# A buffer of their own for layer 0's modulation rows, and four temporaries in place of six

## The chip, the cores and the metric

The kernel runs on one core of a Trainium2 chip. The metric is the device time of one execution, in microseconds (us), as the median of several executions. The engines are named as in the profile: PE (TensorE's matmuls), PEld (its weight loads), DVE (VectorE), ACT (ScalarE), POOL (GpSimd) and SP (SyncE, which issues all the loads and stores here). L129 means line 129 of the kernel.

## What is computed

A bidirectional encoder of two layers over 1024 tokens of width 1024, in float32. Layer 0 mixes tokens by differential attention with 8 heads, layer 1 by grouped-query attention; each has a SwiGLU block behind it. Every norm is modulated by a condition vector: six rows of 1024 numbers per layer come from a product with a large matrix. Cut to layer 0's first half:

```python
cond = silu(c)
mod = (cond @ ada_w[i] + ada_b[i])          # 6 x 1024 per layer
shift1, scale1, gate1, shift2, scale2, gate2 = split(mod, 6)
h = rmsnorm(x, norm1_g[i]) * (1 + scale1) + shift1
q, k, v = split(h @ w_qkv, 3)               # 8 heads; q and k have two halves of 64
q, k = rope(q), rope(k)                     # the first quarter of each half is rotated
w = softmax(q1 k1) - lam * softmax(q2 k2)
y = rmsnorm(w @ v, subln_g) * (1 - lam_init) @ w_o
x = x + gate1 * y
```

## The kernel before

Activations lie as 8 blocks of 128 features by 1024 tokens, worked on in chunks of 512 tokens. A float32 product is made of three matmuls: each operand is split into a rounded high part and the low rest (`split`, L94: a cast on ACT, a subtraction on the engine named, POOL in layer 0 for weights). `weights` (L82) loads a raw tile of 128x1024 (tag `wraw`), then splits it into `whi` and `wlo`; the pool `wp0` has two buffers for each of the three tags.

`start` (L334) loads x and the first two modulation rows' matrices (`aq`, reduced on DVE at L377), normalises x, and projects q, k and v of head 0. `layer0_attn` (L439) then runs 8 heads of 8 query blocks (a head's 64 units are walked by `attention`, L272). While head h is in its scores, softmax and values, the projections of head h+1 are mixed in as fills: six groups of 24 matmuls (`qkv_steps`, L474: q, k and v, two chunks each), each in the one PSUM bank M, which ACT empties at L470 (`evac`) into a temporary `tmp`. For q and k, `rope_fin` (L457) takes a second temporary, shuffles the first into it on DVE (L221), multiplies by the tables and adds (L223 to L225, on POOL for heads above 0), and `pack` splits the result into two tiles of the pool `h`. That pool has 50 tiles of 128x512: 32 hold the layer's input throughout the projections, 8 each the rotated q and k of a head. `subln` (L568) takes two more temporaries for the norm of the output of each half head; the second is stored to memory by SP (L1050).

The other four modulation rows of layer 0 (gate1, scale2, shift2, gate2) are made during the heads by `ada_steps` (L121): 32 steps, four or five to a head, in the fills of heads 0 to 6. A step loads 128x1024 of the matrix, multiplies it by the condition on POOL (L129) and sums it on ACT (L130). Its tile is also a `wraw` of `wp0`, so weights and steps share two buffers. Layer 1 calls the same function.

No order is written out by hand: a planner in the framework goes through the program with its own model of time and writes the list of each engine, taking the instruction of highest priority that is ready; priorities follow the program, lifted for some (`high_priority`). Buffers of a tag are given out in program order, an engine works through its list in order, and SP's list is the order of all the loads and stores.

Of the kernel before, what the change touches and what calls it, by code (L numbers as in the profile page):

```python
# [9 lines left out]
F32 = mybir.dt.float32  # L10
# [44 lines left out]
SH_A = [i ^ 8 if i < 16 else i for i in range(32)]  # L55
# [3 lines left out]
class Trunk:  # L59
# [58 lines left out]
        self.nc.scalar.activation(out=t, in_=t, func=AF.Silu)  # L118
        return t

    def ada_steps(self, layer, j, dst, cond):  # L121

        nc = self.nc

        def step(d):
            w = self.t(self.wp, "wraw")
            nc.sync.dma_start(out=w, in_=self.a["ada_t"][layer, j - 2, d])
            with self.tc.high_priority(offset=DAHEAD):
                nc.gpsimd.tensor_tensor(out=w, in0=w, in1=cond, op=ALU.mult)  # L129
                nc.scalar.activation(out=w, in_=w, func=AF.Copy, accum_out=dst[:, d:d + 1])  # L130
            if d == KT - 1:
                b = C_ADAB + layer * 48 + j * 8
                nc.gpsimd.tensor_tensor(out=dst, in0=dst, in1=self.sm[:, b:b + 8], op=ALU.add)

        return [lambda d=d: step(d) for d in range(KT)]
# [303 lines left out]
    def layer0_attn(self, hs, tiles, od):  # L439
        nc, tc, a = self.nc, self.tc, self.a  # L440
        m = self.mods[0]
        self.wlo = nc.gpsimd
        with tc.tile_pool(name="a_tab", bufs=1, reuse_waits="tile") as tab, \
                tc.tile_pool(name="a_v", bufs=2, reuse_waits="tile") as vp, \
                tc.tile_pool(name="a_tmp", bufs=6, reuse_waits="tile") as tp, \
                tc.tile_pool(name="a_e", bufs=5, reuse_waits="tile") as ep, \
                tc.tile_pool(name="a_p", bufs=6, reuse_waits="tile") as pp:
            cos, sin = self.t(tab, "cos"), self.t(tab, "sin")
# [6 lines left out]
            half = lambda: self.t(tp, "tmp", [P, CH])  # L455

            def rope_fin(h, i, c, z):  # L457
                cs = slice(c * CH, c * CH + CH)
                self.rope(half(), z, cos[:, cs], sin[:, cs], SH_A, z, nc.gpsimd if h else None)
                ready.setdefault((h, i), []).append(self.pack(z))  # L460

            def evac(h, i, c, ps):
                if i == 2:
                    if c == 0:
                        vt[h] = self.t(tab, "vz")
                    z = vt[h][:, c * CH:(c + 1) * CH]
                else:
                    z = half()
                with self.tc.high_priority(offset=MAHEAD):
                    nc.scalar.activation(out=z, in_=ps, func=AF.Copy, scale=0.125 if i == 0 else 1.0)  # L470
                if i < 2:
                    rope_fin(h, i, c, z)
# [19 lines left out]
            ada = []  # L492
            cond = self.condr
            for j in (2, 4, 3, 5):
                ada += self.ada_steps(0, j, m[j], cond)
            fills = []
            wo = self.wo = OutProj(self, a["woA"], od, a["xT"], m[2])
            for h in range(8):
# [704 lines left out]
```

## Time and profile before

| | us |
|---|---|
| median of 3 runs | 2755.31 (2752.56 to 2761.1) |
| profiled execution | 2753.28 |
| its span, first to last instruction | 2751.2 |
| mean granted TensorE clock | 0.97 of full speed |

| engine | busy, share of the span |
|---|---|
| PE | 95% |
| PEld | 78% |
| DVE | 70% |
| ACT | 43% |
| POOL | 36% |

The start lasts until about 72 us, layer 0's heads until about 735 us; then follow layer 0's SwiGLU block, layer 1's heads from about 1480 us and its SwiGLU block. A busy share is a mean over these stages. For a change in one stage, the idle time of PE in that stage is what counts: the stretches of the span give it, and the single instructions show what ended each wait.

### The profile page before, as it was taken

To read this page: it belongs to the slowest core of one execution; us is meant where nothing else is said; L and a number is where in the kernel's file an instruction comes from. 1 tells how busy PE (TensorE), PEld (TensorE's weight loads), DVE (VectorE), ACT (ScalarE), POOL (GpSimd) and SP (SyncE) were. 2 spreads that over 40 slices of the span, in tenths; PEclk is the share of its full clock that TensorE was granted. 3 is DMA by queue.
4 is the path that set the end of the run, shared out by engine and by line. 5 is a ranking of instruction groups with operands and counts; after the bars stand their busy time and mean duration, and the time that the engine had idled before them with its cause. 6 is when DMAs were issued, how large, how long until landed. Compare 5 with 4: busy or idle time off the path is not lost.

```text
span 2751.2 us, 34376 instructions
## 1 busy us (share of the span) xinstructions
PE 2600.1 (95%) x12888; PEld 2138.1 (78%) x12888; DVE 1913.9 (70%) x2921; ACT 1193.2 (43%) x2049; POOL 988.7 (36%) x664
## 2 busy tenths in 40 slices
PE   6799999999998999999999899999998999999997
PEld 5577777777776888888887788888877888888886
DVE  6777777777667667676666777577567666666666
ACT  5455555555443333333334565555443333332323
POOL 7634444531154223232223456433153222222222
PEclk9899999999998999999999999999999999999998
DMA  6211211112211222221214222213211111111112
GB/s 255 74 44 49 70 50 59 63 42 96 78 49 58 66 65 74 65 69 62 71 64 146 96 73 89 85 59 110 70 35 50 54 50 58 54 50 54 50 58 85
DMA packets 86582, 195.89 MB, mean 71 GB/s; under 512 B 9488, under 2 KB 11792, under 8 KB 86416
## 3 DMA queue, kind: packets, MB, share of 16 engines
q1 hardware_dynamic: 86416, 193.71, 20.7%
q8 instruction: 101, 1.65, 0.3%
q14 instruction: 65, 0.53, 0.1%
HBM read 177.94 MB, written 15.73 MB: 70 GB/s over the span
## 4 chain that ended last, share of the span: by engine, by line
PE 76%; DVE 12%; ACT 3%; POOL 3%; DMA 2%; issue 2%; SPq 0%; DVEq 0%; ACTq 0%; POOLq 0%
PE T L105 7%; PE T L106 7%; PE T L107 7%; PE S L106 6%; PE S L105 6%; PE S L107 6%; PE M L105 6%; PE M L106 5%; PE M L107 5%; PE S L548 3%; PE T L256 3%; PE A L270 2%; PE A L268 2%; PE A L269 2%; DVE mx L556 2%
## 5 line engine op out<-in xcount | busy, mean ns | idle before, releaser
L833 POOL TENSOR_TENSOR raw<-raw,raw 128x512 f32<-128x512 f32 x214 | 299.2, 1399 | 877.5 <-DMA raw<-in_w_in 552.1
L95 ACT CAST whi<-raw 128x512 fp32r<-128x512 f32 x402 | 249.0, 621 | 672.1 <-PE T L106 215.7
L96 DVE TENSOR_TENSOR wlo<-raw,whi 128x512 fp32r<-128x512 f32 x402 | 330.3, 826 | 124.8 <-ACT whi L95 124.4
L105 PE MATMUL M<-h,whi 128*128 128x512 f32 x616 | 252.6, 410 | 8.6 <-ACT tmp L470 4.2
L1036 DVE SCALAR_TENSOR_TENSOR h<-T,mod,h 128x512 f32<-128x512 f32 (+1 forms) x270 | 197.7, 733 | 70.8 <-PE T L107 69.6
L107 PE MATMUL M<-h,wlo 128*128 128x512 f32 x616 | 244.6, 397 | 1.0 <-POOL wlo L96 1.0
L105 PE MATMUL S<-h,whi 128*128 128x512 f32 x572 | 226.7, 397 | 19.5 <-DVE ft L918 19.3
L106 PE MATMUL M<-h,whi 128*128 128x512 f32 x616 | 244.9, 398 | 0.0
L95 ACT CAST pt<-T 128x512 fp32r<-128x512 f32 x256 | 145.3, 588 | 211.5 <-PE T L256 211.0
L106 PE MATMUL S<-h,whi 128*128 128x512 f32 x572 | 227.5, 398 | 5.0 <-DVE h L214 3.1
L96 DVE TENSOR_TENSOR pt<-T,pt 128x512 fp32r<-128x512 f32 x256 | 171.6, 682 | 80.7 <-ACT pt L95 80.4
L107 PE MATMUL S<-h,wlo 128*128 128x512 f32 x572 | 226.2, 396 | 0.0
L105 PE MATMUL T<-g,whi 128*128 128x512 f32 (+1 forms) x540 | 210.7, 390 | 10.2 <-DVE h L1036 8.8
L106 PE MATMUL T<-g,whi 128*128 128x512 f32 (+1 forms) x540 | 208.3, 386 | 1.4 <-DVE g L96 1.4
L107 PE MATMUL T<-g,wlo 128*128 128x512 f32 (+1 forms) x540 | 207.9, 385 | 0.0
L129 POOL TENSOR_TENSOR wraw<-wraw,cond 128x1024 f32<-128x1024 f32 x64 | 155.9, 2437 | 126.9 <-DMA wraw<-in_ada_t 119.6
L556 DVE TENSOR_REDUCE mx<-S 128x1 f32<-128x1024 f32 x128 | 150.2, 1215 | 44.3 <-PE S L548 44.2
L270 PE MATMUL A<-pt,v 128*128 128x256 f32 x512 | 155.6, 304 | 23.2 <-DVE pt L96 23.2
L559 ACT ACTIVATE e<-S,mx 128x1024 f32<-128x1024 f32 x128 | 141.4, 1111 | 71.7 <-DVE mx L558 71.7
L256 PE MATMUL T<-ident,e 128*128 128x128 f32 x1024 | 149.1, 280 | 13.3 <-DVE pt L96 10.1
L268 PE MATMUL A<-pt,v 128*128 128x256 f32 x512 | 156.3, 305 | 4.3 <-ACT pt L95 4.2
L269 PE MATMUL A<-pt,v 128*128 128x256 f32 x512 | 151.4, 296 | 0.0
(290 smaller groups left out, 6445.7 us busy)
## 6 DMA issues: line engine op xcount, KB each, us to landing
raw<-in_w_in SPq DMA_DIRECT2D x200, 256.0 KB, 2.8
wraw<-in_ada_t SPq DMA_DIRECT2D x64, 512.0 KB, 3.2
raw<-in_w_out SPq DMA_DIRECT2D x88, 256.0 KB, 2.6
wraw<-in_wqkvA SPq DMA_DIRECT2D x23, 512.0 KB, 3.2
aq<-in_ada_s SPq DMA_DIRECT2D x16, 512.0 KB, 4.9
raw<-in_ada_w SPq DMA_DIRECT2D x32, 256.0 KB, 2.6
wraw<-in_wqkvB SPq DMA_DIRECT2D x15, 512.0 KB, 3.3
o<-tmp SPq DMA_DIRECT2D x28, 256.0 KB, 2.0
```

The costliest lines, as they stand in the source:

```text
L95: self.nc.scalar.copy(out=hi, in_=src)
L96: (eng or self.nc.vector).tensor_tensor(out=lo, in0=src, in1=hi.bitcast(F32), op=ALU.subtract)
L105: mm(ps, lhsT=whi[:, ws], rhs=xh, start=first and k == 0, stop=False)
L106: mm(ps, lhsT=whi[:, ws], rhs=xl, start=False, stop=False)
L107: mm(ps, lhsT=wlo[:, ws], rhs=xh, start=False, stop=last and k == n - 1)
L256: nc.tensor.transpose(ps[:, i * P:(i + 1) * P], w[:, k * P:(k + 1) * P], self.ident)
L268: mm(ps, lhsT=vh[:, ks], rhs=hi, start=(k == 0), stop=False)
L269: mm(ps, lhsT=vl[:, ks], rhs=hi, start=False, stop=False)
L270: mm(ps, lhsT=vh[:, ks], rhs=lo, start=False, stop=(k == KT - 1))
L556: nc.vector.tensor_reduce(out=mx, in_=ps, op=ALU.max, axis=AX.X, negate=True)
L833: self.nc.gpsimd.tensor_tensor(out=t, in0=x, in1=y, op=op)
L1036: self.nc.vector.scalar_tensor_tensor(out=x, in0=ps, scalar=gate2[:, d:d + 1], in1=x, op0=ALU.mult, op1=ALU.add)
```

## The change

The 32 steps of layer 0 take their tiles from the pool `cr`, which held only the condition's row, under a tag of its own with one buffer (4 KB per partition). The weights and the loads of stored outputs keep the two `wraw` buffers. The pool of temporaries of layer 0's attention has four buffers instead of six (4 KB per partition less). The second tile of a rotation comes from the pool `h` instead. Layer 1 is as before.

```diff
-    def ada_steps(self, layer, j, dst, cond):
+    def ada_steps(self, layer, j, dst, cond, pool=None):
 ...
-            w = self.t(self.wp, "wraw")
+            w = self.t(pool, "adaw") if pool else self.t(self.wp, "wraw")
             nc.sync.dma_start(out=w, in_=self.a["ada_t"][layer, j - 2, d])
 ...
-                tc.tile_pool(name="a_tmp", bufs=6, reuse_waits="tile") as tp, \
+                tc.tile_pool(name="a_tmp", bufs=4, reuse_waits="tile") as tp, \
 ...
-                self.rope(half(), z, cos[:, cs], sin[:, cs], SH_A, z, nc.gpsimd if h else None)
+                self.rope(self.hslot(F32), z, cos[:, cs], sin[:, cs], SH_A, z, nc.gpsimd if h else None)
 ...
-                ada += self.ada_steps(0, j, m[j], cond)
+                ada += self.ada_steps(0, j, m[j], cond, self.cpool)
```

## Rows read from the trace of the kernel before

**Rows 1.** The page, part 1: busy us, share of the span, instructions.

```profile
PE 2600.1 (95%) x12888; PEld 2138.1 (78%) x12888; DVE 1913.9 (70%) x2921; ACT 1193.2 (43%) x2049; POOL 988.7 (36%) x664
```

**Rows 2.** Stretches: bounds, length, busy PE, PEld, DVE, ACT, POOL; clock, DMA share, GB/s.

```profile
35.00:72.00 37.00, 35.20 (x139) 26.86 (x140) 28.55 (x63) 14.56 (x21) 28.91 (x16) 0.95 0.49 172
72.00:135.00 63.00, 46.23 (x205) 33.56 (x205) 49.14 (x63) 31.84 (x54) 45.24 (x23) 0.86 0.22 76
135.00:293.00 158.00, 152.42 (x887) 122.81 (x887) 117.13 (x201) 85.22 (x150) 64.06 (x41) 0.96 0.14 51
```

**Rows 3.** The same stretches, L129 alone: bounds, length, POOL busy; clock, DMA.

```profile
35.00:72.00 37.00, 2.40 (x1) 0.95 0.49 172
72.00:135.00 63.00, 14.68 (x6) 0.86 0.22 76
```

**Rows 4.** Instructions on tile wraw, both layers: ns min/median/max, first and last start.

```profile
L129 POOL TENSOR_TENSOR wraw<-wraw,cond x64: 2348/2392/3347, 43.3 to 1862.5; 128x1024 f32<-128x1024 f32 x64
L130 ACT ACTIVATE wraw<-wraw x64: 1043/1060/1086, 48.3 to 1865.0; 128x1024 f32<-128x1024 f32 x64
L130 ACT ACTIVATION_READ_ACCUMULATOR wraw<-wraw x64: 182/186/217, 49.2 to 1866.0; 128x1 f32 x64
...
DMA to landing us min/median/max: 2.6/3.2/10.2
```

**Rows 5.** Timeline of the start: start, us, instruction, [idle before <- what ended it].

```profile
34.99 4.61 POOL L388 TENSOR_SCALAR nh<-h,a,mod 128x512 f32<-128x512 f32 x2 [1.80 <-DVE mod L379]
...
42.06 0.68 DVE L389 TENSOR_TENSOR h<-nh,h 128x512 fp32r<-128x512 f32 x1
...
43.33 2.88 DVE L389 TENSOR_TENSOR h<-nh,h 128x512 fp32r<-128x512 f32 x1 [0.53 <-POOL nh L388]
...
43.27 2.40 POOL L129 TENSOR_TENSOR wraw<-wraw,cond 128x1024 f32<-128x1024 f32 x1
...
51.33 0.50 PE L106 MATMUL S<-h,w0h 128*128 128x512 f32 x1 [0.69 <-DVE h L389]
...
72.55 1.77 POOL L223 TENSOR_TENSOR tmp<-tmp,cos 128x512 f32<-128x512 f32 x1 [4.27 <-DVE tmp L221]
```

**Rows 6.** Timeline of SP's queue in the start.

```profile
34.73 0.38 SPq L127 DMA_DIRECT2D wraw<-in_ada_t  x1
...
49.42 0.38 SPq L86 DMA_DIRECT2D wraw<-in_wqkvA  x1
```

**Rows 7.** Timeline of SP's queue and of ACT, head 1: a weight.

```profile
181.65 0.33 SPq L86 DMA_DIRECT2D wraw<-in_wqkvA  x1
...
193.45 1.05 ACT L95 CAST whi<-wraw 128x1024 fp32r<-128x1024 f32 x1 [0.16 <-PE M L106]
```

**Rows 8.** Timeline of DVE, ACT and PE in the run-in.

```profile
80.05 1.63 DVE L96 TENSOR_TENSOR h<-tmp,h 128x512 fp32r<-128x512 f32 x1
...
86.24 0.62 ACT L95 CAST h<-tmp 128x512 fp32r<-128x512 f32 x1 [7.42 <-DVE tmp L225]
86.77 0.59 ACT L470 ACTIVATE tmp<-M 128x512 f32<-128x512 f32 x1
...
87.41 0.51 PE L105 MATMUL M<-h,whi 128*128 128x512 f32 x1 [2.60 <-ACT tmp L470]
```

**Rows 9.** Two half heads: all engines as in rows 2, then L129 alone.

```profile
336.50:376.80 40.30, 38.65 (x224) 31.51 (x224) 30.34 (x55) 22.99 (x40) 21.64 (x14) 0.96 0.14 46
...
455.60:495.50 39.90, 37.97 (x217) 30.16 (x216) 32.36 (x47) 20.86 (x37) 16.39 (x10) 0.96 0.22 73
...
336.50:376.80 40.30, 3.92 (x2) 0.96 0.14 46
...
455.60:495.50 39.90, 7.90 (x4) 0.96 0.22 73
```

**Rows 10.** Waits of ACT from 135 to 608: us in total, times, longest.

```profile
ACT h L95 <- POOL tmp L225: 8.3, 4, 5.0
```

**Rows 11.** Waits of DVE from 0 to 72: us in total, times, longest.

```profile
DVE aq L377 <- DMA aq<-in_ada_s: 1.2, 1, 1.2
```

## The prediction

> **What bounds the kernel now.** I read the page's busy shares first, then stretches of the span, then the single instructions at the places that the change touches. TensorE is busy for 95% of the span [rows 1], so an edit that touches no matmul can only move TensorE's idle time. Layer 0's attention phase ends near 735 us; everything the change touches lies before that. By stretch [rows 2], TensorE idles 37.00 - 35.20 = 1.8 us in the second half of the start (35 to 72), 63.00 - 46.23 = 16.8 us in the run-in (72 to 135, head 0's rotation and first scores), and 5.6 us in the 158 us behind that. Only the run-in is a place with something to win; the start is a place with almost no cover: whatever becomes late there is late on TensorE.
>
> The modulation rows are 32 loads of 512 KB, each followed by one POOL multiply (L129) and one ACT sum (L130). Of the 32, one is multiplied before 72, six in the run-in [rows 3], and the other 25 behind that. Now they take turns with the q, k, v weights in two buffers, in the order of the program, so a row can't run ahead of the weights.
>
> **Part 1: what the weights gain from their two buffers: nothing.** A weight load issued at 181.65 lands some 3 us later, but its first use, the split on ACT at 193.45, is held by a TensorE matmul that frees the split pair, not by the load [rows 7]. The raw tile has been there for about 8 us. The 0.16 us of idle shows that the split starts the moment the pair is free. An earlier load would wait longer for the same pair. So 0, and the cover is those 8 us.
>
> **Part 2: the rows run ahead.** With a buffer of their own the rows wait for each other alone: load, multiply, sum, next load. One turn is 3.2 us of landing + 2.39 + 1.06 + 0.19 for the sum's read-out + 0.4 for the issue [rows 4, 6], 7.2 us when nothing else is in the way; landings go up to 10.2 us, so I take 8 to 9 us beside the start's loads. The first row is issued in the start as soon as the queue is free. The kernel before shows that the planner does pull rows that far: its row 0 was issued at 34.73, and then nothing more, because the next weight took the freed buffer at 49.42 [rows 6]. Alone, the rows would be multiplied at about 33, 42, 51, 60 and 69 us: five before 72 in place of one.
>
> What one costs is seen at row 0 [rows 5]: POOL multiplies from 43.27 for 2.40 us; VectorE's subtraction of the same shape, which took 0.68 us just before, starts at 43.33 and takes 2.88. That is 2.20 us lost on VectorE, which makes the modulation columns there, and TensorE then waits 0.69 us for VectorE's h and loses more in parts. I price a row in the start so: the first fits in POOL's idle 1.80 us before 34.99, and 2.40 - 1.80 = 0.6 sticks out; the second stands where row 0 stood and costs nothing new; the third and fourth cost 2.2 each; the fifth lies in POOL's idle 4.27 us before 72.55 and is free. Sum 5.0. Bounds: 0 (every row finds such idle time) and 4 x 2.40 = 9.6 (none does). I take 5.0 since POOL is busy 28.91 of 37 us and VectorE 28.55 in that stretch [rows 2].
>
> The other queues that the rows pass: ACT gets four more sums of 1.25 us and is busy 14.56 of 37 us, so 0. On SP's list a row's load waits for the sum of the row before, and the start's own loads stand behind it; VectorE waited for those only once, 1.2 us in all [rows 11], and the DMA share is 0.49, so 0 while a load has some us to spare, and the length of SP's wait if not.
>
> In the run-in the rows already come about as fast as their turn allows (6 in 63 us, while the turn gives 7 or 8). One more, at 2.2, while head 0's rotation is on VectorE: +2.2, between 0 and 4.8.
>
> The Trainium skill has a rule for this place: "SBUF — State Buffer", section "SBUF: two separate sides", says that VectorE operations with two SBUF inputs and GpSimd operations hold a shared port pair exclusively, and that the second one fully waits for the first. By that rule no part of a row is free while VectorE has such an operation next, and the sum for the start would be the upper bound. The 2.88 against 0.68 agrees, but only for a pair of operations that meet; it is the price of my first rival.
>
> **Part 3: four temporaries, the rotation's second tile among the h tiles.** Per head the temporaries were q0, its shuffle, q1, its shuffle, k0, its shuffle, two for the output's norm, k1, its shuffle, two more: twelve on six; now eight on four. In the run-in the six are too few: head 1's first projection waits on TensorE for 2.60 us at 87.41, since its bank M is emptied by ACT only at 86.77, and that ACT copy stands behind a cast that starts at 86.24, after 7.42 us of waiting for the rotation's add [rows 8]. With the shuffles elsewhere a temporary comes free when the first tile is packed, at 80.05 + 1.63 = 81.7, before the matmuls end at 87.41 - 2.60 = 84.8. I take -2.0 (most of 2.60; the cast may still stand ahead of the copy on ACT), between 0 and -2.6. In the later heads the four are enough: by the time that k0 is emptied, q0 has been packed. The h tiles: 32 hold layer 0's input, 8 the head in use, 8 the next, and 2 of 50 remain for the shuffles, which is what the rotation uses at a time. So 0; without these two the rotation would wait for a head's scores to end.
>
> **Part 4: the heads from 135 on.** More rows until about 300, none behind. Two half heads with the same mean clock (0.96) lasted 40.30 us with 2 rows and 39.90 with 4 [rows 9], so rows cost and free nothing there: 0. Bounds: a row that POOL waits for stands ahead of a rotation, and an ACT cast waits for that: this happened 4 times for 8.3 us in all, at most 5.0 [rows 10], with little of it passed to TensorE. With two or three times as many rows in that stretch it could reach +5; -1 if it goes away.
>
> **The sum.** +5.0 + 2.2 - 2.0 + 0 = +5.2 us against the profiled execution of 2753.3 us (span 2751.2 and 2.1 around it): 2758.5. That execution lies 2.0 below the median 2755.3 of the three, so the forecast of the median is 2760.5, rounded to 2760. That is +0.2%; a measurement of this kernel can tell about 0.3% (8.3 us) from no change.
>
> **Rivals.**
> 1. Slower: every row that the planner pulls into the start and the run-in meets VectorE. Place: 26 to 95 us. Price: four more rows in the start at 2.40 and one in the run-in at 2.40 make 12.0, and the relief of part 3 doesn't come, since ACT works in order: 2755.3 + 12.0 = 2767; with part 4's +5 it is 2772. For it: 1.8 us of cover on TensorE in the start, and the 2.20 of row 0. Against it: POOL has idle stretches of 1.80 and 4.27 us there. It decides from four rows at 2.2 without relief, 8.8 us.
> 2. Faster: the run-in shortens. If the rotation of head 0 isn't held by its temporaries, head 1's projection and the first scores come earlier, and half of the 16.8 us of idle goes (8.4); the mean clock there is 0.86, against 0.95 and 0.96 beside it, and half of that 0.1 over 63 us is another 3.2. That is -11.6: 2744. For it: the 2.60 us wait is really one for a temporary. Against it: in the run-in VectorE is busy 49.14 and POOL 45.24 of 63 us, the rows add to both.
> 3. The change doesn't do what it says: the planner leaves the rows where they are, since the lists of POOL and ACT have no earlier gap in its own timeline. Then only part 3 remains: 2753 to 2755.
>
> **How the numbers follow.** Forecast (2753 to 2763, predicted 2760) 0.47; rival 1 (2764 to 2775) 0.35; rival 2 (2740 to 2747) 0.12; rival 3 0.06. Slower by over 0.3% is rival 1: 0.35. Faster is rival 2 and a little: 0.13. Within is the rest, 0.52. The range leaves out about a tenth on each side: 2747 to 2774.
>
> **What would show it.** Count L129 before 72 and before 135: five and twelve or so if part 2 holds, one and seven if rival 3. TensorE's idle in 35 to 72 should grow from 1.8 to some 7 us, and single VectorE operations there should take over 2 us beside an L129. The 2.60 us wait should be gone or below 0.6. Weight splits should still start right behind a TensorE matmul, and half heads should still last about 40 us, with rows or without. It is wrong if the rows pile up in front of the rotation in heads 1 to 3 (ACT's casts waiting for POOL far beyond 8.3 us), if h tiles or four temporaries hold an evacuation of bank M, or if a row at the head of the load queue delays the start's own loads.

## The result, and the profile after

The changed kernel takes 2778.4 us (median of 4; 2772.5 to 2780.1) beside 2753.9 for the kernel before on the same chip: +24.5 us, ratio 1.0082, 95% interval 1.0068 to 1.0096. It is slower, beyond the upper end of the forecast's range. The profiled execution spans 2775.1 us.

The page, part 1, answers to [rows 1]: each engine has the same work as before.

```profile
PE 2597.8 (94%) x12888; PEld 2135.7 (77%) x12888; DVE 1913.1 (69%) x2921; ACT 1194.0 (43%) x2049; POOL 991.9 (36%) x664
```

TensorE's busy time is even 2.3 us shorter than before, and its mean clock over the span is 0.97 in both. What grows is its idle time, from 151.1 us (2751.2 - 2600.1) to 177.3 (2775.1 - 2597.8).

The stretches of [rows 2] after the change, and one behind them, columns as there; then L129 alone (POOL busy; count; clock; DMA share), as [rows 3].

```profile
35.00:72.00 37.00, 30.26 (x118) 22.48 (x118) 33.79 (x63) 15.94 (x23) 31.54 (x18) 0.96 0.50 176
72.00:135.00 63.00, 45.11 (x187) 33.18 (x186) 46.27 (x50) 29.80 (x51) 47.55 (x26) 0.83 0.30 105
135.00:293.00 158.00, 135.42 (x768) 108.41 (x767) 117.69 (x174) 89.33 (x161) 85.12 (x46) 0.92 0.26 89
293.00:608.00 315.00, 301.73 (x1787) 242.83 (x1787) 222.31 (x412) 157.77 (x275) 105.62 (x74) 0.99 0.08 28
...
35.00:72.00 37.00, 5.79 (x3) 0.96 0.50 176
72.00:135.00 63.00, 18.36 (x8) 0.83 0.30 105
135.00:293.00 158.00, 50.78 (x21) 0.92 0.26 89
293.00:608.00 315.00, 2.37 (x1) 0.99 0.08 28
```

The last stretch in the kernel before, all engines and L129 alone:

```profile
293.00:608.00 315.00, 298.87 (x1740) 240.52 (x1737) 239.73 (x394) 170.69 (x301) 143.69 (x89) 0.97 0.17 58
...
293.00:608.00 315.00, 42.88 (x18) 0.97 0.17 58
```

The rows have run ahead: 20 begin in 135 to 293 (the 21st of that line began at 133.3), one behind it where there were 18. TensorE's idle time in 135 to 293 grows from 5.6 us [rows 2] to 22.6 (158.00 - 135.42) and its clock falls from 0.96 to 0.92. Behind 293, where no rows are left, it is busy 2.9 us more than before at a clock 0.02 higher. So the change loses in heads 0 to 2 and gets some of it back later.

How much, and where, is told by the exponentials (ACT L559), of which each block of queries has two: head 0's first starts at 102.2 in the kernel before and at 109.8 after the change, +7.5; at the middle of head 2 the delay is 29.4; at the last unit of head 7 (719.9 and 739.1) it is 19.2; at the end of the span 23.9. So by these times 7.5 us come from the start and the run-in, 22 from heads 0 to 2, some 10 are given back, and the last 5 arise behind layer 0's heads, in work that the change doesn't touch.

The first of these times hides a part. PE alone up to head 0's and head 1's first exponential, first before, then after (bounds, length, busy PE and number of matmuls; clock, DMA share, GB/s):

```profile
0.00:102.20 102.20, 73.66 (x298) 0.92 0.53 194
0.00:181.50 181.50, 141.23 (x660) 0.90 0.37 133
...
0.00:109.80 109.80, 73.46 (x285) 0.89 0.56 207
0.00:198.60 198.60, 143.33 (x658) 0.88 0.42 151
```

At head 0's first exponential the changed kernel is not only 7.5 us late, it has also begun 13 matmuls of head 1's projection fewer; at 0.23 us each that is another 3 us (an estimate). So some 10 us belong to the start and the run-in, and some 19 to heads 0 to 2. At head 1's first exponential the work is nearly equal, and the delay is 17.1 us.

How a row costs there is seen at one place in head 0. The timeline of POOL, ACT, PE and DVE: start, us, instruction, [idle before <- what ended it].

```profile
156.96 3.44 POOL L129 TENSOR_TENSOR adaw<-adaw,cond 128x1024 f32<-128x1024 f32 x1 [4.39 <-DMA adaw<-in_ada_t]
...
160.43 1.06 ACT L130 ACTIVATE adaw<-adaw 128x1024 f32<-128x1024 f32 x1 [4.01 <-POOL adaw L129]
...
161.49 0.57 ACT L573 COPY tmp<-A 128x512 f32<-128x512 f32 x1
162.09 0.63 ACT L574 ACTIVATE tmp<-tmp 128x512 f32<-128x512 f32 x1
...
162.77 1.87 PE L184 MATMUL A<-ones,tmp 128*128 128x1 f32 x8 [3.36 <-ACT tmp L574]
...
164.91 2.38 POOL L129 TENSOR_TENSOR adaw<-adaw,cond 128x1024 f32<-128x1024 f32 x1 [4.51 <-DMA adaw<-in_ada_t]
167.25 1.28 POOL L223 TENSOR_TENSOR tmp<-tmp,cos 128x512 f32<-128x512 f32 x1
...
165.42 1.89 DVE L584 TENSOR_TENSOR sv<-sv,c 128x4 f32<-128x4 f32 x1
```

The row's load lands late, so POOL stands for 4.39 us; ACT has the sum next in its list and stands for 4.01; the output's copy and square are behind it, and TensorE stands for 3.36, of which the copy and the square themselves are 1.2. (In the kernel before, TensorE waits for none of the 16 squares of layer 0.) Then the next row comes: POOL stands again for 4.51 us in front of the rotation's first step, and VectorE's product of 128x4 takes 1.89 us, until that L129 ends.

This gap of TensorE also costs behind its end. PE alone, in the stretches before the gap, behind it and after that: busy PE; clock, DMA share, GB/s.

```profile
150.00:159.40 9.40, 7.27 (x48) 0.96 0.16 58
162.70:168.00 5.30, 5.23 (x17) 0.51 0.24 92
168.00:171.70 3.70, 3.70 (x17) 1.00 0.42 142
```

After the 3.36 us the clock stands at 0.51 of full speed (the level of 1.2 GHz) for 5.3 us, so another 2.6 us of work are lost. Not every gap is followed by that: behind the 2.60 us of [rows 8] the clock in the kernel before is 1.00:

```profile
87.40:92.40 5.00, 4.99 (x22) 1.00 0.11 29
```

Over 135 to 293, the waits of ACT and POOL for the rows, in us, times, longest; first after the change, then in the kernel before:

```profile
ACT adaw L130 <- POOL adaw L129: 28.8, 12, 4.3
...
POOL adaw L129 <- DMA adaw<-in_ada_t: 45.9, 10, 7.4
```

```profile
ACT wraw L130 <- POOL wraw L129: 9.6, 7, 2.5
...
POOL wraw L129 <- DMA wraw<-in_ada_t: 18.6, 5, 4.7
```

### The profile page after: what moved, and what is told of

The parts are those of the page before. It is cut to its first block, busy times and chain, and to the rows that moved or that the text cites. A ratio compares the mean times of both kernels' runs of the same rounds, so it can differ in the third digit from the quotient of the medians.

```text
span 2775.1 us, 34387 instructions
## 1 busy us (share of the span) xinstructions
PE 2597.8 (94%) x12888; PEld 2135.7 (77%) x12888; DVE 1913.1 (69%) x2921; ACT 1194.0 (43%) x2049; POOL 991.9 (36%) x664
## 4 chain that ended last, share of the span: by engine, by line
PE 74%; DVE 13%; ACT 4%; POOL 4%; issue 3%; DMA 2%; SPq 0%; DVEq 0%; ACTq 0%; POOLq 0%
PE T L105 7%; PE T L107 7%; PE T L106 7%; PE S L106 6%; PE S L105 6%; PE S L107 6%; PE M L105 6%; PE M L106 5%; PE M L107 5%; PE S L548 3%; PE T L256 3%; PE A L270 2%; DVE mx L556 2%; PE A L268 2%; DVE wlo L96 2%
## 5 line engine op out<-in xcount | busy, mean ns | idle before, releaser
L105 PE MATMUL M<-h,whi 128*128 128x512 f32 x616 | 256.2, 416 | 9.3 <-DVE tmp L632 2.2
L106 PE MATMUL M<-h,whi 128*128 128x512 f32 x616 | 247.6, 402 | 0.0
L96 DVE TENSOR_TENSOR pt<-T,pt 128x512 fp32r<-128x512 f32 x256 | 172.0, 684 | 83.8 <-ACT pt L95 83.5
L559 ACT ACTIVATE e<-S,mx 128x1024 f32<-128x1024 f32 x128 | 141.7, 1114 | 84.3 <-DVE mx L558 80.2
L270 PE MATMUL A<-pt,v 128*128 128x256 f32 x512 | 152.2, 297 | 26.9 <-DVE pt L96 26.9
L268 PE MATMUL A<-pt,v 128*128 128x256 f32 x512 | 152.2, 297 | 7.8 <-ACT pt L95 5.5
L223 POOL TENSOR_TENSOR tmp<-tmp,cos 128x512 f32<-128x512 f32 x52 | 74.1, 1424 | 214.0 <-DVE h L221 164.9
L256 PEld LDWEIGHTS T<-ident,e 128*128 128x128 f32 x1024 | 120.9, 144 | 37.9 <-issue 11.5
```

The lines of the kernel that those rows point to most:

```text
L96: (eng or self.nc.vector).tensor_tensor(out=lo, in0=src, in1=hi.bitcast(F32), op=ALU.subtract)
L105: mm(ps, lhsT=whi[:, ws], rhs=xh, start=first and k == 0, stop=False)
L106: mm(ps, lhsT=whi[:, ws], rhs=xl, start=False, stop=False)
L256: nc.tensor.transpose(ps[:, i * P:(i + 1) * P], w[:, k * P:(k + 1) * P], self.ident)
L268: mm(ps, lhsT=vh[:, ks], rhs=hi, start=(k == 0), stop=False)
L270: mm(ps, lhsT=vh[:, ks], rhs=lo, start=False, stop=(k == KT - 1))
```

## The experiments

One table holds the readings on which the verdicts rest. "Start" is the time of head 0's first exponential, then each head's time from its first exponential to the next head's; in brackets are the rows multiplied in it; "layer 0" is the time of the last unit's first exponential, "rest" the span behind it. The difference is that of the medians of this kernel and of the kernel before beside it on the same chip; the interval is that of the ratio. The runs of the kernel before lie between 2748 and 2765 us, so a single trace carries about 5 us of its own. "Start" and "head 0" are to be read together, as above: by the first exponential TensorE has begun 285 to 324 matmuls, by kernel (298 before, 319 in e2_temps_alone).

| kernel | difference, us | ratio, 95% interval | start | head 0 | 1 | 2 | 3 | 4 | 5 | 6 | layer 0 | rest |
|---|---|---|---|---|---|---|---|---|---|---|---|---|
| before | | | 102.2 (3) | 79.3 (6) | 77.7 (4) | 79.9 (5) | 78.5 (4) | 80.6 (5) | 78.6 (5) | 78.9 (0) | 719.9 | 2031 |
| after | +24.5 | 1.0068 to 1.0096 | 109.8 (8) | 88.8 (11) | 85.6 (11) | 79.2 (2) | 77.2 (0) | 76.8 (0) | 78.0 (0) | 79.8 (0) | 739.1 | 2036 |
| e2_temps_alone | +1.3 | 0.9993 to 1.0019 | 106.8 (4) | 77.2 (5) | 79.0 (4) | 81.8 (5) | 79.7 (4) | 79.2 (5) | 79.6 (5) | 80.6 (0) | 728.0 | 2031 |
| e3_rows_held | +24.1 | 1.0076 to 1.0107 | 109.1 (6) | 80.1 (4) | 79.2 (4) | 84.7 (5) | 80.4 (4) | 82.8 (5) | 82.8 (4) | 80.7 (0) | 743.3 | 2041 |
| e5_short_multiply | +7.8 | 1.0020 to 1.0043 | 111.1 (11) | 87.6 (16) | 79.2 (5) | 78.2 (0) | 76.7 (0) | 78.5 (0) | 78.1 (0) | 80.5 (0) | 733.7 | 2031 |
| e6_free_sum | +19.5 | 1.0059 to 1.0093 | 118.3 (11) | 82.8 (12) | 89.7 (9) | 78.0 (0) | 76.6 (0) | 78.5 (0) | 78.7 (0) | 80.8 (0) | 746.5 | 2034 |
| e7_both | +9.8 | 1.0020 to 1.0044 | 107.0 (13) | 85.6 (19) | 78.3 (0) | 78.7 (0) | 78.3 (0) | 78.6 (0) | 78.3 (0) | 80.6 (0) | 729.5 | 2038 |
| e8_rows_from_head1 | +7.5 | 1.0017 to 1.0040 | 99.7 (0) | 76.0 (4) | 78.9 (5) | 79.5 (4) | 79.8 (5) | 78.7 (4) | 79.5 (5) | 80.6 (1) | 720.3 | 2048 |
| e9_free_from_head1 | +17.1 | 1.0054 to 1.0087 | 104.4 (3) | 88.8 (11) | 82.2 (11) | 86.5 (7) | 76.7 (0) | 77.1 (0) | 76.7 (0) | 80.2 (0) | 736.6 | 2038 |
| e10_dense | +5.8 | 1.0012 to 1.0035 | 108.5 (5) | 82.4 (10) | 80.5 (8) | 83.0 (8) | 76.6 (1) | 78.3 (0) | 78.3 (0) | 80.5 (0) | 732.4 | 2031 |
| e11_rows_heads1to6 | -0.1 | 0.9984 to 1.0008 | 99.1 (0) | 76.1 (5) | 78.7 (5) | 81.3 (5) | 79.2 (6) | 81.5 (5) | 81.2 (5) | 78.4 (1) | 719.6 | 2034 |
| e12_held_later | +21.3 | 1.0061 to 1.0091 | 104.8 (3) | 82.9 (6) | 79.6 (5) | 82.1 (5) | 82.7 (5) | 82.0 (5) | 81.6 (3) | 80.7 (0) | 740.5 | 2041 |
| e13_held_free_sum | +16.6 | 1.0045 to 1.0075 | 107.0 (4) | 73.9 (4) | 81.4 (6) | 83.7 (4) | 76.6 (6) | 85.2 (4) | 78.0 (4) | 80.1 (0) | 730.4 | 2038 |
| e14_shared_free_sum | +3.9 | 1.0001 to 1.0026 | 109.2 (5) | 73.8 (4) | 77.3 (4) | 80.4 (5) | 78.1 (4) | 79.0 (5) | 78.9 (5) | 80.7 (0) | 720.5 | 2034 |
| e15_behind_split | +10.8 | 1.0029 to 1.0059 | 106.3 (3) | 76.2 (4) | 79.1 (4) | 85.9 (5) | 78.1 (4) | 84.1 (5) | 78.6 (5) | 81.1 (2) | 733.4 | 2041 |
| e16_one_raw | +8.3 | 1.0014 to 1.0049 | 108.2 (4) | 81.7 (5) | 81.7 (4) | 81.8 (5) | 81.5 (4) | 81.6 (5) | 79.2 (5) | 75.4 (0) | 735.7 | 2029 |
| e17_shared_short | -9.3 | 0.9951 to 0.9979 | 101.8 (5) | 73.8 (4) | 78.2 (4) | 79.6 (5) | 79.5 (4) | 76.9 (5) | 78.3 (5) | 80.8 (0) | 712.1 | 2037 |
| e18_held_short | -1.6 | 0.9989 to 1.0014 | 107.1 (5) | 72.1 (4) | 78.2 (5) | 79.0 (5) | 80.6 (5) | 78.0 (5) | 83.8 (3) | 80.3 (0) | 723.3 | 2037 |

The rest needs care. Nothing is edited there (layer 1's rows in e3_rows_held aside), but the planner orders that work in several ways. In the traces, from 100 us behind the last unit on, TensorE's list is one and the same in the kernel before, e10, e11 and e18 (rest 2031 to 2037), in e2, e5, e6 and e16 (2029 to 2034), in e3, e7 and e12 (2038 to 2041), and in e8, e9, e13, e15 and e17 (2037 to 2048); after the change and in e14 it is a list of its own. So some 5 to 10 us of a difference can come from the order of later work and not from the rows. The column "layer 0" is free of that.

**Which part of the change it is.** The first theory (R in the expectations): rows that run ahead stand in front of the heads' work on ACT and POOL. Rivals: the temporaries (T), or the meeting of the multiply with VectorE (C).

e2_temps_alone, made from the changed kernel:

```diff
-                ada += self.ada_steps(0, j, m[j], cond, self.cpool)
+                ada += self.ada_steps(0, j, m[j], cond)
```

> Layer 0's rows take turns with the weights again, as in the kernel before; the four temporaries and the rotation's second tile among the h tiles stay. Theory R (rows that run ahead stand in front of the heads' work on ACT and POOL, in order, and cost all of the change's 24 us): within 4 us of the kernel before, or up to 3 us faster if the 2.60 us wait in the run-in is really for a temporary; L129 back to six or so between 72 and 135, ACT's waits for L129 from 72 to 300 back from 42.6 us to about 10. Theory T (four temporaries, or h tiles taken by the rotation, hold the evacuations): about 2778, with ACT's casts and TensorE's M L105 waiting for tmp.

Measured: +1.3 us (the interval is -2 to +5), no difference that can be measured. The four temporaries and the rotation's tiles in `h` cost nothing and bring nothing that shows; the 24.5 us belong to the rows' buffer. No run has that buffer beside six temporaries, so whether four of them matter only with it isn't tested; but from 100 to 740 in the changed kernel ACT's copies into `tmp` (L470, L573) wait for TensorE's products alone, for 1.8 and 12.7 us, and never for a temporary to come free. The relief in the run-in didn't come either:

```profile
85.19 0.62 ACT L95 CAST h<-tmp 128x512 fp32r<-128x512 f32 x1 [7.08 <-DVE tmp L225]
85.72 0.59 ACT L470 ACTIVATE tmp<-M 128x512 f32<-128x512 f32 x1
...
86.36 0.79 PE L105 MATMUL M<-h,whi 128*128 128x512 f32 x1 [4.60 <-ACT tmp L470]
```

This is the place of [rows 8] in e2_temps_alone (ACT, then PE): the copy out of bank M still stands behind the cast that waits for the rotation, and TensorE's wait is 4.60 us where it was 2.60. What holds the copy is ACT's order, not a temporary.

e3_rows_held, made from the changed kernel (the first line in `weights`; layer 1's rows are held too):

```diff
-        nc.sync.dma_start(out=raw[:, :n], in_=src)
+        self.w_load = nc.sync.dma_start(out=raw[:, :n], in_=src)
 ...
-            nc.sync.dma_start(out=w, in_=self.a["ada_t"][layer, j - 2, d])
+            with self.tc.issue_after(self.w_load.ins): nc.sync.dma_start(out=w, in_=self.a["ada_t"][layer, j - 2, d])
```

> All of the change stays, but each row's load is put on SP's queue behind the weight load that precedes it in the program, so that rows can't run ahead though their buffer is free. Theory R: 2750 to 2757, as before; L129 spread over the seven heads. Theory T: about 2778. If the single row buffer as such (one load, one multiply, one sum in turn) costs, whatever its place in time, then halfway or more of the 24 us stays: 2766 to 2778.

Measured: +24.1 us, and that with four or five rows to a head. So running ahead is not the whole story: a buffer of its own costs as much when the rows are spread. The heads lose one by one (head 2 84.7, heads 4 and 5 82.8). This kernel also holds layer 1's rows, and its rest is 10 us longer than that of the kernel before; layer 0 is 15 us later than in e2_temps_alone.

**The number of rows in a head.** e10_dense and e9_free_from_head1 set the number apart from the buffer (Theory D: the number decides). e10_dense, made from the kernel before:

```diff
-                e = ada[h * 32 // 7:(h + 1) * 32 // 7]
+                e = ada[h * 8:h * 8 + 8]
```

> The kernel before (six temporaries, rows in the weights' buffers), but the rows stand eight to a head in heads 0 to 3. Theory D: heads 0 to 3 take 82 to 87 us each in place of 78 to 80 and heads 4 to 6 about 77 to 78, with the early rows some +10 to +20 us in sum, 2767 to 2777, though rows and weights still share their buffers. If it is the buffer of its own that costs (a row that is due ahead of its load), and not the number in a head: within 5 us of before.

Measured: +5.8 us; heads of 8 to 10 rows take 80.5 to 83.0 us, heads 3 to 5, with one row or none, 76.6 to 78.3. Two of the three dense heads lie in Theory D's range, but the sum is under its +10, and just above the 5 us of the other theory: it lies between them.

e9_free_from_head1, made from the changed kernel (with `self.w_load` as in e3_rows_held):

```diff
+            with self.tc.issue_after(self.w_load.ins) if pool and j == 2 and d == 0 else contextlib.nullcontext(): nc.sync.dma_start(out=w, in_=self.a["ada_t"][layer, j - 2, d])
 ...
-                e = ada[h * 32 // 7:(h + 1) * 32 // 7]
+                e = ada[(h - 1) * 32 // 7:h * 32 // 7] if h else []
```

> As the changed kernel, but the rows stand in the fills of heads 1 to 7 and the first row's load is queued behind the first weight load ahead of it in the program; from there they run ahead freely. Theory D: first scores within 2 us of before (102 to 107 us), 10 or 11 rows to a head in heads 0 to 2 at 85 to 89 us each, then heads of 77 us: +12 to +20 us, 2767 to 2778. If only the start and the run-in cannot bear rows: 2750 to 2760.

Measured: +17.1 us with a start of 104.4, in time as Theory D has it. So the start and the run-in are the place of the smaller part of the loss, 7 of 24.5 us. Heads of eleven rows take 82.2 and 88.8 us there, where one of ten in shared buffers takes 82.4: the number in a head is only a part.

**What a row does where it runs ahead.** Two cuts on the changed kernel. e5_short_multiply:

```diff
-                nc.gpsimd.tensor_tensor(out=w, in0=w, in1=cond, op=ALU.mult)
+                k = 64 if pool else S
+                nc.gpsimd.tensor_tensor(out=w[:, :k], in0=w[:, :k], in1=cond[:, :k], op=ALU.mult)
```

> As the changed kernel, but L129 multiplies only 64 of the 1024 columns in layer 0: the rest of that product is left out. Load, the wait for it, and ACT's sum stay. Theory R by the wait for the load and by order: most of the loss stays, 2765 to 2778, since ACT and POOL stand as long for a load that is late; what goes is the 2.2 us per meeting on VectorE. Theory C (the multiply and VectorE meet, rival 1 of the prediction: 20 rows before 215 at some 1 to 2 us each): 2745 to 2758, with VectorE's subtractions near 0.68 us in the start.

Measured: +7.8 us. The 2767.2 us lie in Theory R's range; but the kernel before took 2759.4 beside it, 5.5 more than beside the changed kernel, and as a difference the result lies between the two theories: 17 of the 24.5 us go with the multiply's length, although the rows now come faster (27 before the end of head 0 in place of 19). The cut shortens POOL's own work as well as the meeting with VectorE, so it doesn't part the two.

e6_free_sum:

```diff
-                nc.scalar.activation(out=w, in_=w, func=AF.Copy, accum_out=dst[:, d:d + 1])
+                r = w if not pool else self.sm[:, C_FG:C_FG + 8]
+                nc.scalar.activation(out=self.t(self.sp, "scr", [P, 8]) if pool else w, in_=r, func=AF.Copy, accum_out=dst[:, d:d + 1])
```

> As the changed kernel, but ACT's sum in layer 0 reads 8 unrelated columns, so it waits for no multiply and takes little time: the sum over the row is left out. The rows are multiplied on POOL as before, with no wait of ACT behind them, and may run ahead still further. Theory R by ACT's order (a sum that waits for a late row holds the exponentials, casts and copies behind it): 2755 to 2768, with TensorE's idle in 135 to 215 down from 15.8 us to 6 or so. Theory C, or a loss by POOL's own waits for loads: 2770 to 2778.

Measured: +19.5 us. ACT's waits for L129 are gone, and yet the time stays: the rows come earlier still, and the start is at 118.3. TensorE's idle time in 135 to 215 does shrink, from 15.8 us to 9.8 (forecast: 6 or so). Theory R by ACT's order falls as the whole cause.

e7_both has both edits:

> As the changed kernel, with both of the last call's cuts for layer 0: L129 multiplies 64 of 1024 columns (the rest of the product is left out), and ACT's sum reads 8 unrelated columns and waits for no multiply (the sum over the row is left out). The rows' loads and POOL's wait for them stay, at a still faster pace. If the meeting with VectorE and ACT's wait in order are the two causes: 2750 to 2760, heads 0 and 1 at 77 to 81 us. If POOL's own waits for the loads hold the rotations behind them: 2764 to 2775, with POOL's waits for the rows' loads above 50 us in all and TensorE's idle in heads 0 and 1 as in the changed kernel.

Measured: +9.8 us, as e5_short_multiply, and in the range of POOL's waits. With 19 rows in head 0 that head still takes 85.6 us: POOL waits there 18 times, 51.5 us in all, for the rows' loads. The rotation stands behind them, and behind it the power in the output's norm (POOL, 166.44), for which TensorE waits:

```profile
167.72 2.08 PE L192 MATMUL A<-ident,sr 128*128 128x128 f32 x8 [9.02 <-DVE sr L591]
```

**The start and head 7.** e8_rows_from_head1, made from the kernel before:

```diff
-                e = ada[h * 32 // 7:(h + 1) * 32 // 7]
+                e = ada[(h - 1) * 32 // 7:h * 32 // 7] if h else []
```

> The kernel before (six temporaries, rows in the weights' buffers), with the 32 rows mixed into the fills of heads 1 to 7 instead of 0 to 6; none left for the start and the run-in, four or five in each head. Theory D (what a row costs depends on how many lie in one head and whether the place has slack: some 1.2 us each ahead of the first scores, read from 106.8 us with 4 rows against 109.1 with 6 there, and under 0.5 us each at four or five to a head): first scores 3 to 6 us earlier, 2748 to 2756 beside a before of about 2757 on that chip. Against it, a theory in which a row costs the same wherever it lies: no change within 2 us.

Measured: +7.5 us, though the start is 2.5 us earlier than in the kernel before and head 0 another 3.3. Both sides of the expectation fall: of the 5.8 us, 3.1 are left when head 7 begins, none at its last unit, and the rest is 17 us longer. Four rows lie in head 7 now. TensorE's waits there, from 650 to 760, us in total, times, longest:

```profile
PE T L105 <- ACT g L95: 4.5, 1, 4.5
PE M L105 <- DVE h L1068: 4.3, 2, 2.9
```

Neither of them is among the waits of e2_temps_alone in that stretch. The rows took turns with the output projection's weights there; that the work behind them came late by it is argued, and some of the 17 us may come from TensorE's order in the rest, which e9, e13, e15 and e17 share (2037 to 2041).

e11_rows_heads1to6 has `e = ada[max(h - 1, 0) * 32 // 6:h * 32 // 6]` in that line:

> The kernel before (six temporaries, rows in the weights' buffers), with the 32 rows mixed into the fills of heads 1 to 6, five or six in each: none ahead of the first scores, where a row cost some 1.2 to 1.8 us, and none in head 7, where those of the last call held the loads and splits of the output projection's weights. Theory D: first scores near 100 us, six heads at 78 to 81 us, head 7 and SwiGLU 0 as in before: 4 to 8 us faster than before, 2751 to 2756 beside some 2759. If the last call's gain ahead of the first scores is given back later whatever lies in head 7: within 2 us of before.

Measured: -0.1 us. The start is again 3 us earlier, at 99.1, and head 0 is 76.1; with five or six rows each, heads 2, 4 and 5 take it back. No placing of the rows that was tried beats the kernel before.

**A buffer of its own at the old pace.** e12_held_later (Theory P: with two buffers of their own the weights are loaded early, and rows queued behind them come early too) is e3_rows_held for layer 0 alone, with the rows placed later in the program:

```diff
-                e = ada[h * 32 // 7:(h + 1) * 32 // 7]
+                e = []
 ...
+            for i, r in enumerate(ada):
+                fills[5 + i * 51 // 32].append(r)
```

> As e3_rows_held (own buffer, each row's load behind the last weight load ahead of it in the program; here in layer 0 alone, layer 1 as in the changed kernel), but the rows stand in the program five units (about two weights) later, evenly from unit 5 to unit 55. Theory P (with buffers of their own the weights are loaded up to two weights ahead of their use, so a row queued behind such a load comes up to 26 us too early, ahead of the rotation instead of behind the scores): layer 0 as in before or a few us better, 2750 to 2760. If the single row buffer itself costs at any place in time: heads 2, 4 and 5 at 82 to 85 us again, 2766 to 2776.

Measured: +21.3 us; each of heads 0 to 5 is 1 to 4 us longer than in the kernel before. Theory P by that shift falls.

e13_held_free_sum and its control e14_shared_free_sum cut ACT's sum as in e6_free_sum, in e12_held_later and in e2_temps_alone (Theory O: the sums stand at worse places in ACT's list):

> As e12_held_later (own buffer, the rows' pace held by the weight loads, so that the number in a head stays at five or so), but ACT's sum for layer 0 reads 8 unrelated columns and waits for no multiply (the sum over the row is left out). Theory O (with the buffer of its own, the sums stand in ACT's list where the row isn't there yet, and the exponentials and copies behind them are late): of the 20 us that e12_held_later lost to the kernel before by the end of layer 0, at least 10 go; 2758 to 2768. If the loss lies with POOL's wait for loads and VectorE: 2774 to 2782.

> The control for the run beside it: e2_temps_alone (rows share the weights' buffers, four temporaries) with the same cut of ACT's sum in layer 0 (the sum over the row is left out). Theory O: sharing already keeps the sums where their rows are there, so ACT's sums cost little: 2753 to 2760, within 5 us of e2_temps_alone. If the sum itself costs wherever it stands: 8 us or more faster than e2_temps_alone, 2745 to 2752.

Measured: +16.6 us against e12_held_later's +21.3 (layer 0 ends 10 us earlier), and +3.9 for the control, whose layer 0 also ends 7.5 us earlier than in e2_temps_alone. The first lies between the two theories. The order on ACT is a part at most: in the medians 4.7 us, with intervals that overlap.

e16_one_raw is e3_rows_held for layer 0 alone, and gives layer 0's raw weights one buffer:

```diff
+        kw = {"bufs": 1} if tag == "wraw" and pool.name == "wp0" else {}
```

> As e3_rows_held for layer 0 alone (own row buffer, four temporaries, each row's load queued behind the last weight load ahead of it), but layer 0's raw weights have one buffer instead of two, so a weight is loaded only when the one before it has been split, and the rows come later with it. Theory P (the moment at which the rows come costs, not their buffer): heads 1 to 6 in 77 to 82 us each, SwiGLU 0 and layer 1 as in before; 2752 to 2762, some 3 us of it for a start that loads its weights one at a time. If the buffer of its own costs at any moment: 2772 to 2782.

e15_behind_split, made from the changed kernel (`self.w_lo` is kept in `weights`):

```diff
+            g = nc.sync.dma_start(out=self.t(self.sp, "gate", [1, 8]), in_=self.w_lo.bitcast(F32)[0:1, 0:8]) if pool else None
+            with self.tc.issue_after(g.ins) if g else contextlib.nullcontext():
+                nc.sync.dma_start(out=w, in_=self.a["ada_t"][layer, j - 2, d])
```

> As the changed kernel, but ahead of each row of layer 0 SP issues a copy of 32 bytes out of the last weight's low part, so the row's load is queued behind that weight's finished split (as it is where rows and weights share buffers). Theory P: no row ahead of 72, four or five to a head, heads 1 to 6 in 77 to 82 us each; 2753 to 2764. If SP's wait for the split holds the weights' loads behind it, TensorE waits for M L106 or L107 in each head: 2765 to 2785. If the buffer of its own costs at any moment: 2772 to 2782 with no such waits.

Measured: +8.3 and +10.8 us, between the theories (TensorE has no wait for bank M from 135 to 736 in e15_behind_split, so its second theory's condition isn't met): making the rows come later, as the shared buffers do, gives back about half of the 21 to 24 us, with the buffer of its own kept. In layer 0 alone e12_held_later ends 12.5 us behind e2_temps_alone, these two 7.7 and 5.4. So about half of it is the moment at which the rows come, as far as two edits show that also take a buffer from the weights or put a copy on SP's list.

**The multiply at the old pace.** The last two runs cut the multiply as in e5_short_multiply, in e2_temps_alone and in e12_held_later.

> e2_temps_alone (rows share the weights' buffers, four temporaries) with L129 of layer 0 multiplying 64 of the 1024 columns (the rest of the product is left out). Price of a row by the meeting with VectorE: in the kernel before, VectorE's operations that overlap an L129 lie 37 us over their usual length in all, for 32 rows; if all of that reached TensorE, 2720; if the cover holds a half or more, 2738 to 2756. Prediction's part 4 (rows cost and free nothing in the heads) would have it at 2750 to 2760.

> e12_held_later (own buffer, the rows' pace held by the weight loads) with the same cut of the multiply in layer 0. If the own buffer's 21 us are the meeting with VectorE at worse moments: within 5 us of e17_shared_short beside it. If they are order and waits: 15 to 20 us above it, as e12_held_later stands to e2_temps_alone.

Measured: -9.3 and -1.6 us. The first fits the cover of a half or more and part 4 alike; the second is 7.7 us above it, between its two cases. In the medians the cut is worth 10.6 us with shared buffers (0.33 us a row) and 22.9 us with the buffer of its own (0.72 a row), and of the 20 us between e2_temps_alone and e12_held_later 7.7 stay.

The traces don't find this in the heads. There the cut brings layer 0's last unit 15.8 us forward with shared buffers and 17.2 with the buffer of its own, some 0.5 us a row in both, and the own buffer costs 12.5 us with the full multiply and 11.2 with the short one. What makes the medians differ lies in the rest: 2031 and 2037 us with shared buffers, 2041 and 2037 with the own, each time with another order of TensorE's list. So the multiply's length costs something wherever the rows lie; that it is what the buffer of its own costs at the old pace is not shown, and what does cost there stays open.

Single waits do grow with the buffer of its own, those for the values' product above all. From 135 to 736: in turn e2_temps_alone, e12_held_later, e17_shared_short and e18_held_short (in the last two the line is one further):

```profile
PE A L270 <- DVE pt L96: 17.5, 13, 1.4
```

```profile
PE A L270 <- DVE pt L96: 20.9, 13, 3.9
...
PE A L184 <- ACT tmp L576: 7.0, 3, 2.9
```

```profile
PE A L271 <- DVE pt L96: 14.7, 13, 1.7
```

```profile
PE A L271 <- DVE pt L96: 14.1, 13, 2.1
PE A L269 <- ACT pt L95: 8.6, 7, 2.1
```

With shared buffers, none of the 13 waits is over 1.4 us. With the buffer of its own there are waits of 3.9 us and, for ACT's square, of 2.9. With the short multiply none is over 2.1, but others have come: the 8.6 us for ACT were 1.6 in e12_held_later. How a long wait comes about is seen in e3_rows_held, half way through head 5 (POOL and DVE, then PE):

```profile
549.27 2.41 POOL L129 TENSOR_TENSOR adaw<-adaw,cond 128x1024 f32<-128x1024 f32 x1
...
554.61 2.36 POOL L96 TENSOR_TENSOR wlo<-wraw,whi 128x1024 fp32r<-128x1024 f32 x1 [1.68 <-ACT whi L95]
...
550.33 1.38 DVE L579 TENSOR_SCALAR top<-s 128x4 f32<-128x4 f32 x1 [0.67 <-ACT e L559]
...
555.12 2.40 DVE L96 TENSOR_TENSOR h<-tmp,h 128x512 fp32r<-128x512 f32 x1
557.44 2.34 DVE L556 TENSOR_REDUCE mx<-S 128x1 f32<-128x1024 f32 x2
...
560.56 0.58 PE L270 MATMUL A<-pt,v 128*128 128x256 f32 x1 [4.00 <-DVE pt L96]
```

A row just ahead of the rotation's last step holds VectorE's 128x4 operation until 551.7; the rotated tile's subtraction then falls beside the weight's split on POOL and takes 2.40 us; two maxima of 2.34 us stand behind it in VectorE's list; so VectorE comes late to the transposed softmax weights (`pt`), and TensorE stands for 4.00 us. What places the rows is seen in SP's waits of the same stretch, in e2_temps_alone and then in e12_held_later:

```profile
SPq L127 <- POOL wlo L96: 176.4, 16, 17.3
SPq L86 <- ACT wraw L130: 91.8, 15, 7.7
```

```profile
SPq L86 <- POOL wlo L96: 242.4, 20, 22.5
...
SPq L127 <- ACT adaw L130: 71.6, 10, 8.4
```

With shared buffers 16 of the rows' loads wait for a weight's split and 15 of the weights' loads for a row's sum, so the two streams keep out of each other's way. With a buffer of its own no row waits for a split itself; it only stands in SP's list behind weights' loads that do.

## Why the prediction was wrong, and where it was right

**Part 1, the weights' two buffers: 0.** They brought nothing, as forecast. But the two buffers had a second use that the part didn't see: taking turns was what placed the rows among POOL's other work.

**Part 2, the rows run ahead.** This was right in kind. Forecast were five rows before 72 and twelve before 135; there are three (33.1, 49.9 and 62.6), a fourth at 72.4, and eleven before 135. TensorE's idle in 35 to 72 was to be about 7 us; it is 37.00 - 30.26 = 6.7. The price of a meeting was to be 2.2 us; it is seen again:

```profile
62.57 2.36 POOL L129 TENSOR_TENSOR adaw<-adaw,cond 128x1024 f32<-128x1024 f32 x1
...
62.64 2.84 DVE L389 TENSOR_TENSOR h<-nh,h 128x512 fp32r<-128x512 f32 x1
...
65.53 0.50 PE L106 MATMUL S<-h,w0h 128*128 128x512 f32 x1 [1.87 <-DVE h L389]
```

Start and run-in were to cost 5.0 + 2.2 = 7.2; head 0's first exponential is 7.5 us later. That the two are so near is in part luck: TensorE's idle time grows by 4.9 us in 35 to 72 (forecast 5.0, but for five rows; the first three were priced at 2.8) and by 1.1 in 72 to 135 (forecast 2.2), the clock there falls from 0.86 to 0.83, which the sum had no term for, and 3 us of work are left undone. Without rows there (e8, e11), the first exponential comes at 99.7 and 99.1, with 296 matmuls begun in place of 298. What failed in this part is "ACT sums ... so 0": a share of busy time can't say what a sum that waits holds behind it in ACT's order.

**Part 3: -2.0.** It failed: e2_temps_alone measures no difference, and the 2.60 us wait, 4.60 there and 2.12 in the changed kernel (at 94.27; gone or below 0.6 was forecast), is one for ACT's order. The part had the reason against itself in brackets (the cast may still stand ahead of the copy) and yet took most of the 2.60.

**Part 4: 0, at most +5.** This is the step that broke the forecast: it took rows in the heads as free. Heads 0 to 2 lost some 20 us, and the heads without rows gave some 10 back. (The other 5 lie in the rest, for which the sum had nothing.) It argued from two half heads with 2 and 4 rows [rows 9] that rows cost and free nothing. Both ends were too near to each other. After the change, the first halves of heads 1 and 3 are these (bounds, length, busy PE; clock, DMA share, GB/s), the one with six rows, the other with none:

```profile
198.60:243.60 45.00, 39.54 (x214) 0.89 0.25 88
363.50:402.90 39.40, 37.76 (x224) 1.00 0.06 21
```

Between none and four rows the difference is hard to see among 40 us; with six, and loads that POOL waits for, it is 5.6. Even at the old places the multiply alone is worth 10.6 us in the medians (e17_shared_short). And the bound of +5 was taken from one kind of wait [rows 10], where three came together: POOL for the load, ACT for POOL, VectorE for the multiply's end. That one kind grew as the prediction's own sign of being wrong had it, from 8.3 to 16.9 us in the same stretch; but it doesn't measure the loss, since it is 24.7 in e17_shared_short, the fastest of all. The clock fell behind some of the gaps, 0.96 to 0.92 in 135 to 293, and rose again where there were no rows.

**The rivals.** Rival 1 had the resource (the multiply meets VectorE: cutting its length, which relieves POOL too, takes 17 of the 24.5 us away) and the sign, but put it at 26 to 95 us, where the loss is 7.5 to 10; its 2767 to 2772 lies under the result. Rival 2 and rival 3 didn't come: the run-in is longer, and the planner did move the rows.

The rule of the Trainium skill that the prediction cited ("SBUF — State Buffer", section "SBUF: two separate sides") is borne out beyond the pair of [rows 5]: beside an L129, VectorE's product of 128x4 (L584, two inputs) takes 1.89 us. The 1.38 us of L579, shown above too, come from an operation with one input, a case that the prediction's words leave out. What the sum made of the rule, that most of the meetings are covered, held for the old places of the rows: there the whole multiply is worth 0.33 us a row, where a meeting in the start costs 2.2.

**What stays open.** What the own buffer costs at the old pace, 12.5 us in layer 0, of which the later moment gives back about half. And the rest behind layer 0's heads, between 2029 and 2041 us (e8_rows_from_head1 aside): it goes with the order that the planner gave to that work, but no run takes order and rows apart.

## What to carry to other kernels

Buffers that two streams share may be what paces one of them: before giving a side stream a buffer of its own, ask what it waits for now, and which engine will stand in its list when it comes early. The cost of side work is read from heads with none, some and many of it, not from two that are alike; and on in-order engines its price is the queue behind its waits, not its busy time alone. A change in one stage can also change the planner's order in later ones: a difference of a few us is read stage by stage.

## What the hardware showed that was not expected

A gap on TensorE can be paid twice: after 3.36 us without work the clock stood at 0.51 for 5.3 us, and in e2_temps_alone, behind the 4.60 us gap, matmuls of 128x512 followed each other every 0.43 us in place of 0.23 for some 5 us; behind the 2.60 us gap in the kernel before it stood at 1.00. Over the whole span the changed kernel still lost no more clock than the kernel before (0.97 in both). And VectorE's smallest operations can wait as long for POOL as its large ones: the `mod` sum of 128x1 at 50.05, beside the L129 of 49.90, takes 2.36 us where the median of its line is 0.16.

```profile
49.90 2.49 POOL L129 TENSOR_TENSOR adaw<-adaw,cond 128x1024 f32<-128x1024 f32 x1
...
50.05 2.36 DVE L379 TENSOR_TENSOR mod<-mod,sm 128x1 f32<-128x1 f32 x1
```
